# Two w_out chunks and two w_ple_gate chunks as pairs, with seven products for eight in three of eight pairs of k-tiles

## The chip, the core and the metric

The kernel runs on one core of one Trainium2 chip. The time is device microseconds (us) of one execution; lower is better. A core has engines that each work through a list of instructions of their own, in order: PE (TensorE) multiplies matrices, DVE (VectorE) and ACT (ScalarE) work element by element, POOL (GpSimd) does little here, and SP (SyncE) issues transfers between the chip's main memory and the core's own. An instruction waits until what it reads is ready and what it overwrites is no longer needed; whatever stands behind it in the same list waits with it.

## What is computed

One transformer layer for 256 tokens of width 2048, in float32. Cut to what matters here:

```python
z = split_cols(h @ w_in[i])
# three kinds of attention give o_fox, o_nsa, o_dsa
g_fox, g_nsa, g_dsa = jnp.split(jax.nn.sigmoid(z['gate']), 3, axis=-1)
mixed = (g_fox * (o_fox.reshape(B, S, -1) @ w_br_fox[i])
         + g_nsa * (o_nsa.reshape(B, S, -1) @ w_br_nsa[i])
         + g_dsa * (o_dsa.reshape(B, S, -1) @ w_br_dsa[i]))
h = layer_norm(ALPHA * h + mixed @ w_out[i], ln1_g[i], ln1_b[i])
a, b = jnp.split(h @ w_ffn_in[i], 2, axis=-1)
h = layer_norm(ALPHA * h + (jax.nn.silu(a) * b) @ w_ffn_out[i], ln2_g[i], ln2_b[i])
h = h + (p[i] @ w_ple_in[i]) * jax.nn.sigmoid(h @ w_ple_gate[i])
```

The matrices `w_out` and `w_ple_gate` are 2048x2048. Both their products are worked in four chunks of 512 output columns.

## The kernel before

**Halves.** A float32 product is made of three: each operand is split by `halves` into a high half (an ACT copy to the type `fp32r`, L144) and a low half (a DVE subtraction, L145), and PE adds high x high, low x high and high x low in its accumulator (L212 to L214). Weights come as `raw` tiles of two 128-row k-tiles, 128x1024, loaded by SP (L155 in `weight_group`); their halves are `whi` and `wlo`. The matmul that reads a `wlo` is the third of its three, so PE can start a tile with `whi` alone and needs `wlo` two matmuls later.

**One chunk at a time.** `gemm` makes 512 columns for all 256 tokens: 16 k-tiles, two halves of 128 tokens, three matmuls each: 96 matmuls 128x512. Its results lie in two accumulators `acc`. `w_out` runs so in `add_and_norm`: four chunks; after each the residual is added straight from the accumulator (`residual`, L881, a scalar_tensor_tensor on DVE that writes `y`) and its statistics are taken. After chunk 1 come the parameters of the norm and `gated_input`, two small products with `w_ple_in`. `w_ple_gate` runs so in a loop at the end of `build`: after each chunk ACT takes the sigmoid (L1042), DVE multiplies by `ple` (L1043) and adds `y` (L1044), and SP stores.

**Two chunks at a time.** `pair_gemm` makes two chunks of 512 columns at once, and takes the 16 k-tiles by pairs, p = 0 to 7. A pair of k-tiles is a 2x2 matter: two k-tiles, two halves of the tokens, two chunks. In an ordinary pair it takes eight products of three matmuls. In a pair that is in `F.pairs`, here `SEVEN` = (2, 4, 6), it takes seven, by sums and differences of the blocks: 5 x 24 + 3 x 21 = 183 matmuls instead of 192. The differences of the weights are made by DVE (L278 to L280, tiles `raw`), and all are split into halves (`wd`, three blocks wide, and two `wt`); the sums of the other operand are made once by `Forms.put` (tiles `xs`, split into `xf`) and serve every chunk. Four of the seven products gather in accumulators of their own, `m[1]`, `m[5]`, `m[6]`, `m[7]`, over the three seven-pairs; behind the last seven-pair ACT copies `m[1]` and DVE adds the others (L298 to L301, tiles `g`), while PE goes on with the next ordinary pair; at the very end the four ordinary accumulators are added (L305). In the kernel before, the gate chunks (`two_gates`) and 20 of 22 chunks of `w_ffn_in` (`next_chunk`) run in this way, 39 seven-pairs in all.

**What sets the order.** The program writes the steps one after the other, and a scheduler puts them into each engine's list, ahead of their place in the text where their operands and a free buffer allow it. Buffers come from rotating pools: `raw`, `whi`, `wlo` from `wp`, `raw8` of the pairs from a pool of their chunk, wide tiles of the tag `k4` from `k4` and `k4b`. A load waits until its buffer's last reader is done, and SP issues loads in order.

Of the kernel before, what the change touches and what calls it, by code (L numbers as in the profile page):

```python
# [10 lines left out]
F32 = mybir.dt.float32  # L11
# [20 lines left out]
SEVEN = (2, 4, 6)  # L32
# [89 lines left out]
def build(ctx: ExitStack, tc: tile.TileContext, A: dict):  # L122
# [120 lines left out]
    def pair_gemm(a, b, X, F, kt, pool, banks):  # L243
# [15 lines left out]
        def split(src, name, pool, n, **kw):  # L259
            hi, lo = (pool.tile([P, n, 512], F32R, name=f"w{name}{x}", tag=f"w{name}{x}", **kw) for x in ("hi", "lo"))  # L260
            halves(src, hi, lo)
            return [(hi[:, i, :], lo[:, i, :]) for i in range(n)]

        for p in range(np_):
            raw = pool.tile([P, 4, 512], F32, name="raw8", bufs=3)
            nc.sync.dma_start(raw[:, 0:2, :], b[:, 2 * p:2 * p + 2, :])
            nc.sync.dma_start(raw[:, 2:4, :], a[:, 2 * p:2 * p + 2, :])
            x = [[tuple(t[:, hs[h]] for t in X(2 * p + k)) for k in range(2)] for h in range(2)]
            if p not in F.pairs:
                w = [split(raw[:, 2:4, :], "", wp, 2), split(raw[:, 0:2, :], "", wp, 2)]  # L270
# [7 lines left out]
            DVE.tensor_tensor(t[0], raw[:, 0:1, :].broadcast_to([P, 2, 512]), raw[:, 1:3, :], op=ALU.subtract)  # L278
            DVE.tensor_sub(t[1][:, 0, :], raw[:, 1, :], t[0][:, 1, :])
            DVE.tensor_sub(t[1][:, 1, :], raw[:, 3, :], t[1][:, 0, :])  # L280
            b22, b11, b21 = split(raw[:, 1:4, :], "d", pool, 3, bufs=1)
            t3, t1 = split(t[0], "t", pool, 2)
            t2, t4 = split(t[1], "t", pool, 2)
# [11 lines left out]
            if stop:  # L295
# [5 lines left out]
                DVE.tensor_add(e[0][:, 1, :], e[0][:, 1, :], m[5])  # L301
            tick()
        for h in range(2):
            for j in range(2):
                DVE.tensor_add(e[h][:, j, :], e[h][:, j, :], c[h][j])  # L305
# [524 lines left out]
    def two_gates(n):  # L830

        e = pair_gemm(A["gate"][n], A["gate"][4 + n], X, F, KT, gq, (acc_tile, sc_tile))
        for h in range(2):
            ACT.activation(e[h], e[h], AF.Sigmoid)
# [4 lines left out]
        return {"fox": [t[:, 0, :] for t in e], "nsa": [t[:, 1, :] for t in e], "dsa": [g[:, h, :] for h in range(2)]}  # L839

    mixT = Halves()
    for n in range(4):
        G = two_gates(n) if n else {name: [g[:, h, :] for h in range(2)] for name, g in G0.items()}
        if n == 3:
# [6 lines left out]
            halves(mix2, *mixT.t[2])  # L851
        mix = None
# [69 lines left out]
    def add_and_norm(src, X, kt, old, params_of, extra, T, long, spare, first=None):  # L922

        stats = new_stats()
        for n in range(4):
# [29 lines left out]
    def x_tile(n):  # L955
# [7 lines left out]
                 lambda: gated_input(k4, 0, ep), later, LONG1, [k4] * (LONG1 - 4))  # L963
# [15 lines left out]
    def next_chunk(c, pool, banks):  # L979
        e = pair_gemm(A["ffn_in"][c], A["ffn_in"][11 + c], hT, F, KT, pool, banks)  # L980
        for h in range(2):
            ACT.activation(e[h][:, 0, :], e[h][:, 0, :], AF.Silu)
# [111 lines left out]
```

## Time and profile before

| | us |
|---|---|
| median of three runs | 1592.51 |
| the three runs | 1591.29, 1592.51, 1595.47 |
| the profiled execution | 1591.16 |
| its span, first to last instruction | 1589.4 |
| PE busy in the span | 1577.2 (99%) |
| DVE busy | 1110.2 (70%) |
| ACT busy | 785.2 (49%) |

The profile is one execution. Its own time lies 1.76 us above its span and 1.35 us below the median of the three runs. "Busy" is the time in which an engine had an instruction under way. Matmuls overlap: one begins before the last has ended, so what a matmul costs is read from the distance between the starts of two, not from its duration; the same holds, to a lesser degree, for instructions of DVE and ACT. Views used below: the page; the waits (who waited, for what, how long in all, how often, the longest); the windows (busy time of each engine in a stretch); the timeline (each instruction with start and duration, and in brackets the idle time ahead of it).

In the span, the products with `w_br_*` of the last chunk end at about 678 us, those with `w_out` fill 676 to about 775, `w_ffn_in` and `w_ffn_out` follow, and `w_ple_gate` runs from about 1500 to the end at 1589.4.

### The profile page before, as it was taken

To read this page: it belongs to the slowest core of one execution; us is meant where nothing else is said; L and a number is where in the kernel's file an instruction comes from. 1 tells how busy PE (TensorE), PEld (TensorE's weight loads), DVE (VectorE), ACT (ScalarE), POOL (GpSimd) and SP (SyncE) were. 2 spreads that over 40 slices of the span, in tenths; PEclk is the share of its full clock that TensorE was granted. 3 is DMA by queue.
4 is the path that set the end of the run, shared out by engine and by line. 5 is a ranking of instruction groups with operands and counts; after the bars stand their busy time and mean duration, and the time that the engine had idled before them with its cause. 6 is when DMAs were issued, how large, how long until landed. Compare 5 with 4: busy or idle time off the path is not lost. (4 is left out here: it accounts for less than half of the span.)

```text
span 1589.4 us, 19951 instructions
## 1 busy us (share of the span) xinstructions
PE 1577.2 (99%) x7464; PEld 1316.6 (83%) x7464; DVE 1110.2 (70%) x1451; ACT 785.2 (49%) x961; POOL 19.0 (1%) x40
## 2 busy tenths in 40 slices
PE   9999999999999999999999999999999999999998
PEld 7778899988888888888788888888888888888787
DVE  5678565554877777556878888888889664544854
ACT  5445455554544545444455555555555544433443
POOL 1000000000000001000000000000000000000000
PEclk9999999999999999999999999999999999999999
DMA  8665644576475655777565656656665976666474
GB/s 273 221 212 170 195 130 128 163 245 217 145 248 166 222 165 184 219 229 218 164 215 203 207 203 224 219 205 202 223 224 179 299 237 197 195 195 201 144 231 131
DMA packets 92754, 319.72 MB, mean 201 GB/s; under 512 B 10608, under 2 KB 11760, under 8 KB 92656
## 3 DMA queue, kind: packets, MB, share of 16 engines
q1 hardware_dynamic: 91376, 314.25, 61.5%
q0 software_dynamic: 1280, 4.20, 1.0%
q8 instruction: 58, 0.95, 0.2%
q14 instruction: 40, 0.33, 0.1%
HBM read 311.58 MB, written 6.82 MB: 200 GB/s over the span
## 5 line engine op out<-in xcount | busy, mean ns | idle before, releaser
L145 DVE TENSOR_TENSOR wlo<-raw,whi 128x1024 fp32r<-128x1024 f32 (+3 forms) x478 | 564.3, 1187 | 393.4 <-ACT whi L144 389.6
L144 ACT ACTIVATE whi<-raw 128x1024 fp32r<-128x1024 f32 (+3 forms) x478 | 492.7, 1032 | 625.3 <-PE acc L213 360.4
L212 PE MATMUL acc<-whi,k4h 128*128 128x512 f32 (+3 forms) x1388 | 533.2, 384 | 1.5 <-ACT k4h L144 1.4
L213 PE MATMUL acc<-whi,k4l 128*128 128x512 f32 (+3 forms) x1388 | 526.2, 379 | 0.6 <-DVE k4l L145 0.6
L214 PE MATMUL acc<-wlo,k4h 128*128 128x512 f32 (+3 forms) x1388 | 525.8, 379 | 0.0
L212 PEld LDWEIGHTS acc<-whi,k4h 128*128 128x128 f32 x1388 | 261.0, 188 | 51.0 <-issue 4.3
L214 PEld LDWEIGHTS acc<-wlo,k4h 128*128 128x128 f32 x1388 | 260.8, 188 | 45.2 <-DVE wlo L145 0.4
L213 PEld LDWEIGHTS acc<-whi,k4l 128*128 128x128 f32 x1388 | 261.2, 188 | 44.7 <-DVE k4l L145 1.3
L255 PE MATMUL acc<-whi,k4h 128*128 128x512 f32 x320 | 125.2, 391 | 0.0
L257 PE MATMUL acc<-wlo,k4h 128*128 128x512 f32 x320 | 124.9, 390 | 0.0
L256 PE MATMUL acc<-whi,k4l 128*128 128x512 f32 x320 | 124.6, 389 | 0.0
L144 ACT ACTIVATE wthi<-raw 128x1024 fp32r<-128x1024 f32 x78 | 82.1, 1054 | 34.0 <-DVE raw L280 24.6
L145 DVE TENSOR_TENSOR wtlo<-raw,wthi 128x1024 fp32r<-128x1024 f32 x78 | 92.1, 1217 | 0.0
L145 DVE TENSOR_TENSOR wdlo<-raw,wdhi 128x1536 fp32r<-128x1536 f32 x39 | 68.4, 1755 | 16.9 <-ACT wdhi L144 16.5
L255 PE MATMUL sc<-whi,k4h 128*128 128x512 f32 x200 | 78.3, 391 | 0.0
L257 PE MATMUL sc<-wlo,k4h 128*128 128x512 f32 x200 | 77.9, 389 | 0.0
L256 PE MATMUL sc<-whi,k4l 128*128 128x512 f32 x200 | 77.8, 389 | 0.0
L144 ACT ACTIVATE wdhi<-raw 128x1536 fp32r<-128x1536 f32 x39 | 58.1, 1490 | 29.1 <-PE acc L256 15.5
L257 PEld LDWEIGHTS acc<-wlo,k4h 128*128 128x128 f32 x320 | 60.1, 188 | 12.4
L256 PEld LDWEIGHTS acc<-whi,k4l 128*128 128x128 f32 x320 | 60.1, 188 | 12.3
L255 PEld LDWEIGHTS acc<-whi,k4h 128*128 128x128 f32 x320 | 60.1, 188 | 12.1
L278 DVE TENSOR_TENSOR raw<-raw 128x1024 f32<-128x1024 f32 x39 | 47.5, 1219 | 6.2 <-DMA raw<-ffn_in 5.4
(307 smaller groups left out, 1483.4 us busy)
## 6 DMA issues: line engine op xcount, KB each, us to landing
raw<-ffn_in SPq DMA_DIRECT2D x176, 512.0 KB, 4.4
raw<-gate SPq DMA_DIRECT2D x96, 512.0 KB, 4.4
raw<-ffn_out SPq DMA_DIRECT2D x88, 512.0 KB, 4.3
raw<-att_c SPq DMA_DIRECT2D x40, 512.0 KB, 4.4
raw<-att_f SPq DMA_DIRECT2D x48, 384.0 KB, 3.3
raw<-w_out SPq DMA_DIRECT2D x32, 512.0 KB, 4.1
raw<-ple_gate SPq DMA_DIRECT2D x32, 512.0 KB, 4.2
g<-cmp SPq DMA_DIRECT2D x16, 512.0 KB, 5.1
```

The lines of the kernel that those rows point to most:

```text
L144: ACT.activation(hi, src, AF.Copy)
L145: DVE.tensor_sub(lo, src, hi.bitcast(F32))
L212: PE.matmul(o, xh[:, c], h, start=(k == 0), stop=False)
L213: PE.matmul(o, xl[:, c], h, start=False, stop=False)
L214: PE.matmul(o, xh[:, c], l, start=False, stop=(k == kt - 1))
L255: PE.matmul(o, xh, h, start=first, stop=False)
L256: PE.matmul(o, xl, h, start=False, stop=False)
L257: PE.matmul(o, xh, l, start=False, stop=stop)
L278: DVE.tensor_tensor(t[0], raw[:, 0:1, :].broadcast_to([P, 2, 512]), raw[:, 1:3, :], op=ALU.subtract)
```

## The change

The first two chunks of `w_out` (0 and 1) and the middle two of `w_ple_gate` (1 and 2) now run by `pair_gemm`. For `w_out` the seven-pairs are (1, 3, 5), for `w_ple_gate` (2, 4, 6). In these two calls (`slots` is given) the weights of a seven-pair lie in tiles of the shared pools `k4` and `k4b`: each raw load is a tile of its own (`rawb` for the second chunk, `rawa` for the first), the one 1024-wide difference becomes two 512-wide ones, and the 1536-wide split of `wd` becomes a 512-wide (`whl`) and a 1024-wide one. `Forms` of `mixT` are made in the last chunk of the mixing, ahead of its `w_br` products; those of `h2T` behind chunk 0 of `w_ple_gate`. For `w_out` a function `mid` adds the residual to each of the four sums behind the last seven-pair, ahead of the ordinary accumulators; statistics, parameters and `gated_input` come after the pair. The gate of an output block is now the function `gated`. In the other uses of `pair_gemm` one sigmoid 1024 wide becomes two 512 wide; `next_chunk` is only written otherwise.

```diff
--- before.py
+++ after.py
@@ -29,7 +29,7 @@
 LONG1, LONG2, LONG3 = 8, 7, 5
 WARM = 9
 
-SEVEN = (2, 4, 6)
+SEVEN, SEVEN_MIX = (2, 4, 6), (1, 3, 5)
 
 STAY, AHEAD = 2, 1
 NCMP = 15
@@ -240,7 +240,8 @@
         def __call__(self, p, j):
             return self.t[p][:, 0, j, :], self.t[p][:, 1, j, :]
 
-    def pair_gemm(a, b, X, F, kt, pool, banks):
+    def pair_gemm(a, b, X, F, kt, pool, banks, mid=None, slots=None):
...
 
         def split(src, name, pool, n, **kw):
-            hi, lo = (pool.tile([P, n, 512], F32R, name=f"w{name}{x}", tag=f"w{name}{x}", **kw) for x in ("hi", "lo"))
+            tag = "k4" if pool is slots else f"w{name}%s"
+            hi, lo = (pool.tile([P, n, 512], F32R, name=f"w{name}{x}", tag=tag.replace("%s", x), **kw) for x in ("hi", "lo"))
             halves(src, hi, lo)
             return [(hi[:, i, :], lo[:, i, :]) for i in range(n)]
 
         for p in range(np_):
-            raw = pool.tile([P, 4, 512], F32, name="raw8", bufs=3)
-            nc.sync.dma_start(raw[:, 0:2, :], b[:, 2 * p:2 * p + 2, :])
-            nc.sync.dma_start(raw[:, 2:4, :], a[:, 2 * p:2 * p + 2, :])
+            if slots:
+                rb, ra = (slots.tile([P, 2, 512], F32, name=f"raw{x}", tag="k4") for x in "ba")
+            else:
+                raw = pool.tile([P, 4, 512], F32, name="raw8", bufs=3)
+                rb, ra = raw[:, 0:2, :], raw[:, 2:4, :]
+            nc.sync.dma_start(rb, b[:, 2 * p:2 * p + 2, :])
+            nc.sync.dma_start(ra, a[:, 2 * p:2 * p + 2, :])
             x = [[tuple(t[:, hs[h]] for t in X(2 * p + k)) for k in range(2)] for h in range(2)]
             if p not in F.pairs:
-                w = [split(raw[:, 2:4, :], "", wp, 2), split(raw[:, 0:2, :], "", wp, 2)]
+                w = [split(ra, "", wp, 2), split(rb, "", wp, 2)]
                 for h in range(2):
                     for j in range(2):
                         for k in range(2):
@@ -275,12 +281,22 @@
                 tick()
                 continue
             t = [wp.tile([P, 1024], F32, name="raw", bufs=3).rearrange("p (k w) -> p k w", k=2) for _ in range(2)]
-            DVE.tensor_tensor(t[0], raw[:, 0:1, :].broadcast_to([P, 2, 512]), raw[:, 1:3, :], op=ALU.subtract)
-            DVE.tensor_sub(t[1][:, 0, :], raw[:, 1, :], t[0][:, 1, :])
-            DVE.tensor_sub(t[1][:, 1, :], raw[:, 3, :], t[1][:, 0, :])
-            b22, b11, b21 = split(raw[:, 1:4, :], "d", pool, 3, bufs=1)
-            t3, t1 = split(t[0], "t", pool, 2)
-            t2, t4 = split(t[1], "t", pool, 2)
+            if slots:
+                DVE.tensor_sub(t[0][:, 0, :], rb[:, 0, :], rb[:, 1, :])
+                DVE.tensor_sub(t[0][:, 1, :], rb[:, 0, :], ra[:, 0, :])
+            else:
+                DVE.tensor_tensor(t[0], raw[:, 0:1, :].broadcast_to([P, 2, 512]), raw[:, 1:3, :], op=ALU.subtract)
+            DVE.tensor_sub(t[1][:, 0, :], rb[:, 1, :], t[0][:, 1, :])
+            DVE.tensor_sub(t[1][:, 1, :], ra[:, 1, :], t[1][:, 0, :])
+            if slots:
+                hl = slots.tile([P, 2, 512], F32R, name="whl", tag="k4")
+                halves(rb[:, 1, :], hl[:, 0, :], hl[:, 1, :])
+                b22 = hl[:, 0, :], hl[:, 1, :]
+                b11, b21 = split(ra, "d", slots, 2)
+            else:
+                b22, b11, b21 = split(raw[:, 1:4, :], "d", pool, 3, bufs=1)
+            t3, t1 = split(t[0], "t", slots or pool, 2)
+            t2, t4 = split(t[1], "t", slots or pool, 2)
             first, stop = not m, p == last
             for n in (1, 5, 6, 7):
                 if first:
@@ -299,10 +315,11 @@
                 DVE.tensor_add(e[1][:, 0, :], e[0][:, 1, :], m[7])
                 DVE.tensor_add(e[1][:, 1, :], e[1][:, 0, :], m[5])
                 DVE.tensor_add(e[0][:, 1, :], e[0][:, 1, :], m[5])
+                e = [[(mid or (lambda h, j, o: o))(h, j, e[h][:, j, :]) for j in range(2)] for h in range(2)]
             tick()
         for h in range(2):
             for j in range(2):
-                DVE.tensor_add(e[h][:, j, :], e[h][:, j, :], c[h][j])
+                DVE.tensor_add(e[h][j], e[h][j], c[h][j])
         return e
 
     class Halves:
@@ -831,12 +848,13 @@
 
         e = pair_gemm(A["gate"][n], A["gate"][4 + n], X, F, KT, gq, (acc_tile, sc_tile))
         for h in range(2):
-            ACT.activation(e[h], e[h], AF.Sigmoid)
+            for j in range(2):
+                ACT.activation(e[h][j], e[h][j], AF.Sigmoid)
         ps = gemm(A["gate"][8 + n], X, KT, 512)
         g = g_tile()
         for h in range(2):
             ACT.activation(g[:, h, :], ps[h], AF.Sigmoid)
-        return {"fox": [t[:, 0, :] for t in e], "nsa": [t[:, 1, :] for t in e], "dsa": [g[:, h, :] for h in range(2)]}
+        return {"fox": [t[0] for t in e], "nsa": [t[1] for t in e], "dsa": [g[:, h, :] for h in range(2)]}
 
     mixT = Halves()
     for n in range(4):
@@ -849,6 +867,9 @@
             k4b = part.enter_context(tc.tile_pool(name="k4b", bufs=10, reuse_waits="tile"))
             mixT.add(k4b)
             halves(mix2, *mixT.t[2])
+            F = Forms(k4, k4, SEVEN_MIX)
+            for p in SEVEN_MIX:
+                F.put(p, mixT)
         mix = None
         for name, kt, k0 in (("dsa", 6, 10), ("nsa", 4, 0), ("fox", 6, 4)):
             ps = gemm(A["br_" + name][n], lambda k: O(k0 + k), kt, 512)
@@ -919,10 +940,23 @@
             DVE.scalar_tensor_tensor(y, y, rstd, gb[n][:, 1, :], op0=ALU.mult, op1=ALU.add)
             to_dmajor(T, 4 * n, y, h)
 
-    def add_and_norm(src, X, kt, old, params_of, extra, T, long, spare, first=None):
+    def add_and_norm(src, X, kt, old, params_of, extra, T, long, spare, first=None, pair=None):
 
         stats = new_stats()
-        for n in range(4):
+        if pair:
+            o = [old(j) for j in range(2)]
+
+            def mid(h, j, e):
+                DVE.scalar_tensor_tensor(Y[h][j], o[j][h], ALPHA, e, op0=ALU.mult, op1=ALU.add)
+                return Y[h][j]
+
+            pair(mid)
+            for h in range(2):
+                for j in range(2):
+                    DVE.bn_stats(stats[h][:, j, :], Y[h][j])
+            gb = params_of()
+            extra()
+        for n in range(2 if pair else 0, 4):
             o = old(n)
             if n < 3:
                 ps = gemm(src[n], first if first and n == 0 else X, kt, 512)
@@ -960,7 +994,8 @@
     E = []
     later = Later(k4)
     add_and_norm(A["w_out"], mixT, KT, x_tile, lambda: params("ln1_g", "ln1_b", k4b),
-                 lambda: gated_input(k4, 0, ep), later, LONG1, [k4] * (LONG1 - 4))
+                 lambda: gated_input(k4, 0, ep), later, LONG1, [k4] * (LONG1 - 4),
+                 pair=lambda mid: pair_gemm(A["w_out"][0], A["w_out"][1], mixT, F, KT, None, (acc_tile, sc_tile), mid, k4))
     hT = later.x
 
 
@@ -978,10 +1013,10 @@
 
     def next_chunk(c, pool, banks):
         e = pair_gemm(A["ffn_in"][c], A["ffn_in"][11 + c], hT, F, KT, pool, banks)
-        for h in range(2):
-            ACT.activation(e[h][:, 0, :], e[h][:, 0, :], AF.Silu)
-            DVE.tensor_mul(e[h][:, 0, :], e[h][:, 0, :], e[h][:, 1, :])
-        return [e[h][:, 0, :] for h in range(2)]
+        for g, u in e:
+            ACT.activation(g, g, AF.Silu)
+            DVE.tensor_mul(g, g, u)
+        return [g for g, _ in e]
 
     spilled = {}
 
@@ -1029,20 +1064,31 @@
     add_and_norm(A["ffn_out"], actT, 44, lambda n: (Y[0][n], Y[1][n]), lambda: params("ln2_g", "ln2_b", k4),
                  lambda: gated_input(k4, 2, k4), later, LONG2, [k4b] * (LONG2 - 4), first=act_first)
     h2T = later.x
-    for n in range(4):
-        kw = {}
-        if n == 0:
-            kw = dict(sizes=[[2] * LONG3], spare=[k4b] * (LONG3 - 4))
-        elif n == 3:
-            kw = dict(sizes=[[2]] * 5 + [[2, 2, 2]], parts=2)
+
+    def gated(n, h, c, s, o):
+
+        ACT.activation(s, o, AF.Sigmoid)
+        DVE.tensor_mul(s, s, E[n][:, h, c])
+        DVE.tensor_add(s, s, Y[h][n][:, c])
+        nc.sync.dma_start(A["out"][h, :, n * 512 + c.start:n * 512 + c.stop], s)
+
+    F = Forms(k4b, k4b, SEVEN)
+    for n in (0, 1, 3):
+        if n == 1:
+            e = pair_gemm(A["ple_gate"][1], A["ple_gate"][2], h2T, F, KT, None, (acc_tile, sc_tile), slots=k4b)
+            for h in range(2):
+                for j in range(2):
+                    gated(1 + j, h, slice(0, 512), e[h][j], e[h][j])
+            continue
+        kw = dict(sizes=[[2]] * 5 + [[2, 2, 2]], parts=2) if n else dict(sizes=[[2] * LONG3], spare=[k4b] * (LONG3 - 4))
         ps = gemm(A["ple_gate"][n], h2T, KT, 512, **kw)
         s = g_tile()
         w = 512 // (len(ps) - 1)
         for h, c, o in [(0, slice(0, 512), ps[0])] + [(1, slice(i * w, (i + 1) * w), o) for i, o in enumerate(ps[1:])]:
-            ACT.activation(s[:, h, c], o[:, :c.stop - c.start], AF.Sigmoid)
-            DVE.tensor_mul(s[:, h, c], s[:, h, c], E[n][:, h, c])
-            DVE.tensor_add(s[:, h, c], s[:, h, c], Y[h][n][:, c])
-            nc.sync.dma_start(A["out"][h, :, n * 512 + c.start:n * 512 + c.stop], s[:, h, c])
+            gated(n, h, c, s[:, h, c], o[:, :c.stop - c.start])
+        if n == 0:
+            for p in SEVEN:
+                F.put(p, h2T)
 
 
 # ---- launch: one core; the arrays laid out as the kernel loads them ----
```

**DVE in the first two chunks of w_out.** Before, from chunk 0 to the residual of chunk 1 (`wlo`: low halves of weights; `y`: the residual):

```order
L145 TENSOR_TENSOR wlo<-raw,whi 128x1024 x7
L881 SCALAR_TENSOR_TENSOR y<-xt,acc 128x512 x2
L882 BN_STATS stats_5923<-y 128x6
L882 BN_STATS stats_5924<-y 128x6
L145 TENSOR_TENSOR wlo<-raw,whi 128x1024 x8
L881 SCALAR_TENSOR_TENSOR y<-xt,acc 128x512 x2
```

Now, at the end of pair 5, the last seven-pair (`wtlo`: low halves of its differences; `g`: the sums of `m`; the first `wlo` is pair 6's):

```order
L145 TENSOR_TENSOR wtlo<-raw,wthi 128x1024
L950 SCALAR_TENSOR_TENSOR y<-xt,g 128x512
L145 TENSOR_TENSOR wtlo<-raw,wthi 128x1024
L314 TENSOR_TENSOR g<-g,sc 128x512
L315 TENSOR_TENSOR g<-g,sc 128x512
L316 TENSOR_TENSOR g<-g,sc 128x512
L317 TENSOR_TENSOR g<-g,sc 128x512
L950 SCALAR_TENSOR_TENSOR y<-xt,g 128x512 x3
L145 TENSOR_TENSOR wlo<-rawa,whi 128x1024
L145 TENSOR_TENSOR wlo<-rawb,whi 128x1024
```

Four sums and three residuals now stand between the last `wtlo` of the seven-pair and the first `wlo` of the pair that follows it on PE.

**ACT at the change from chunk 0 to chunk 1 of w_ple_gate.** Before (`g<-acc` is the sigmoid of chunk 0):

```order
L144 ACTIVATE k4h<-sc 128x4x128 x3
L144 ACTIVATE whi<-raw 128x1024
L144 ACTIVATE k4h<-sc 128x4x128
L144 ACTIVATE whi<-raw 128x1024 x5
L1042 ACT_TABLE_LOAD
L1042 ACTIVATE g<-acc 128x512 x2
```

Now (`xf`: the halves of the forms; `rawa`, `rawb`: the weights of the pair):

```order
L144 ACTIVATE whi<-raw 128x1024 x2
L144 ACTIVATE xf<-xs 128x512 x3
L1070 ACT_TABLE_LOAD
L1070 ACTIVATE g<-acc 128x512 x2
L144 ACTIVATE whi<-rawa 128x1024
L144 ACTIVATE whi<-rawb 128x1024
```

Three of the five `whi` that stood ahead of the sigmoid were chunk 1's; now none of the pair's stands ahead of it.

**DVE at the same place.** Before:

```order
L145 TENSOR_TENSOR wlo<-raw,whi 128x1024
L145 TENSOR_TENSOR k4l<-sc,k4h 128x4x128
L145 TENSOR_TENSOR wlo<-raw,whi 128x1024 x5
L1043 TENSOR_TENSOR g<-g,ple 128x512 x2
L1044 TENSOR_TENSOR g<-g,y 128x512 x2
L145 TENSOR_TENSOR wlo<-raw,whi 128x1024 x8
```

Now:

```order
L145 TENSOR_TENSOR xf<-xs,xf 128x512
L1071 TENSOR_TENSOR g<-g,ple 128x512 x2
L1072 TENSOR_TENSOR g<-g,y 128x512 x2
L145 TENSOR_TENSOR wlo<-rawa,whi 128x1024
L145 TENSOR_TENSOR wlo<-rawb,whi 128x1024
```

The first `wlo` of the pair stands behind the gate of chunk 0, where three of chunk 1 stood ahead of it. At the end of the last seven-pair of this pair of chunks, pair 6, DVE has the same four sums (L314 to L317) ahead of the first `wlo` of pair 7, without residuals.

## Rows read from the trace of the kernel before

**Rows 1.** The page: busy time of each engine, share of the span, instructions.

```profile
PE 1577.2 (99%) x7464; PEld 1316.6 (83%) x7464; DVE 1110.2 (70%) x1451; ACT 785.2 (49%) x961; POOL 19.0 (1%) x40
```

**Rows 2.** Waits of PE, the longest: us in total, times, longest.

```profile
PE sc L535 <- DVE ra L528: 1.7, 1, 1.7
```

**Rows 3.** Windows: length, busy PE, PEld, DVE, ACT, POOL, clock, DMA share, GB/s.

```profile
1000.00:1100.00 100.00, 100.00 (x452) 82.87 (x451) 87.46 (x89) 55.91 (x57) 0.00 (x0) 1.00 0.63 216
1510.00:1520.00 10.00, 10.00 (x45) 8.26 (x44) 6.04 (x7) 6.32 (x8) 0.00 (x0) 1.00 0.75 227
1580.00:1589.40 9.40, 4.81 (x39) 4.53 (x37) 3.08 (x6) 1.36 (x3) 0.00 (x0) 1.00 0.16 58
```

**Rows 4.** Waits of DVE from 640 to 735 us, around the first w_out chunks.

```profile
DVE wlo L145 <- ACT whi L144: 40.6, 30, 3.0
```

**Rows 5.** Timeline of PE, a gate pair: start, duration, engine, instruction.

```profile
608.79 0.39 PE L255 MATMUL acc<-whi,k4h 128*128 128x512 f32 x1
...
611.96 0.39 PE L257 MATMUL acc<-wlo,k4h 128*128 128x512 f32 x1
612.19 0.39 PE L255 MATMUL sc<-wdhi,k4h 128*128 128x512 f32 x1
```

**Rows 6.** Timeline of DVE, end of one ffn pair of chunks.

```profile
1024.87 1.22 DVE L145 TENSOR_TENSOR wlo<-raw,whi 128x1024 fp32r<-128x1024 f32 x1
...
1028.27 0.68 DVE L298 TENSOR_TENSOR g<-g,acc 128x512 f32<-128x512 f32 x1
...
1030.67 0.68 DVE L300 TENSOR_TENSOR g<-g,acc 128x512 f32<-128x512 f32 x1
1031.27 0.68 DVE L301 TENSOR_TENSOR g<-g,acc 128x512 f32<-128x512 f32 x1
```

**Rows 7.** Timeline of PE there: last into m[6]; later the next pair.

```profile
1026.06 0.39 PE L257 MATMUL acc<-wtlo,xf 128*128 128x512 f32 x1
...
1028.10 0.39 PE L257 MATMUL sc<-wlo,k4h 128*128 128x512 f32 x1
```

**Rows 8.** Timeline of DVE: two differences, the second reads the first.

```profile
1000.73 0.69 DVE L279 TENSOR_TENSOR raw<-raw,raw 128x512 f32<-128x512 f32 x1
1001.45 0.69 DVE L280 TENSOR_TENSOR raw<-raw,raw 128x512 f32<-128x512 f32 x1
```

**Rows 9.** Timeline of DVE: a scalar_tensor_tensor and what follows it.

```profile
1503.06 0.75 DVE L918 SCALAR_TENSOR_TENSOR y<-y,mv,gb 128x512 f32<-128x512 f32 x1
1503.72 1.22 DVE L145 TENSOR_TENSOR wlo<-raw,whi 128x1024 fp32r<-128x1024 f32 x1
```

**Rows 10.** Timeline of ACT, end of w_ple_gate chunk 0.

```profile
1516.99 1.28 ACT L1042 ACT_TABLE_LOAD   x1
1518.29 1.15 ACT L1042 ACTIVATE g<-acc 128x512 f32<-128x512 f32 x2
```

**Rows 11.** Timeline of DVE at the same place.

```profile
1508.84 2.57 DVE L145 TENSOR_TENSOR wlo<-raw,whi 128x1024 fp32r<-128x1024 f32 x2 [0.29 <-ACT whi L144]
...
1518.92 1.30 DVE L1043 TENSOR_TENSOR g<-g,ple 128x512 f32<-128x512 f32 x2 [0.69 <-ACT g L1042]
...
1521.34 1.22 DVE L145 TENSOR_TENSOR wlo<-raw,whi 128x1024 fp32r<-128x1024 f32 x1
```

**Rows 12.** Timeline of PE: last matmul of w_ple_gate chunk 0, then chunk 1.

```profile
1518.41 0.39 PE L214 MATMUL acc<-wlo,k4h 128*128 128x512 f32 x1
1518.64 0.39 PE L212 MATMUL acc<-whi,k4h 128*128 128x512 f32 x1
...
1519.09 0.39 PE L214 MATMUL acc<-wlo,k4h 128*128 128x512 f32 x1
```

**Rows 13.** Tile xs, forms: count, ns min/median/max, first and last start.

```profile
L232 DVE TENSOR_TENSOR xs<-k4h,k4l x6: 678/682/683, 423.0 to 795.5; 128x512 f32<-128x512 f32 x6
L234 DVE TENSOR_TENSOR xs<-xs x6: 281/283/292, 425.0 to 801.1; 128x128 f32<-128x128 f32 x6
```

**Rows 14.** The page: loads of w_out, KB each, median us to landing.

```profile
raw<-w_out SPq DMA_DIRECT2D x32, 512.0 KB, 4.1
```

## The prediction, made before the changed kernel ran

> **What bounds the kernel now.** I read the page first: PE is busy 99% of the span [rows 1]. The waits say how little it lacks anything: its longest single wait is 1.7 us, early in attention [rows 2]. The windows say the same of the stretches that matter: PE is busy all of 1000 to 1100 us, where pairs of `w_ffn_in` chunks run, and all of 1510 to 1520 us in `w_ple_gate`, at a granted clock of 1.00, the 2.4 GHz level [rows 3]. So the time is the number of matmuls times their spacing, plus whatever makes PE wait. DVE is the engine to watch: in the pairs it is busy 87% [rows 3], while around the first `w_out` chunks it waits 40.6 of 95 us for the `whi` of ACT [rows 4]. It has room there on average. The question is what stands in its list at the moments when PE needs something.
>
> **What is saved.** Two pairs of chunks, three seven-pairs each, three matmuls less in each: 18 matmuls. Fifteen spacings lie between 608.79 and 612.19, so one is 0.2267 us [rows 5], and 18 are 4.1 us. A wrong spacing would matter little: the Trainium skill, page "TensorE: Matmul & The Clock Gate", section "Wait — 56ns, not 53.3ns?", gives 0.2157 us for 512 columns at the full clock. By that the saving would be an estimated 3.9 us; the row is measured here and stands. The seven-pairs' differences, splits and the three forms cost DVE and ACT time, which is free as long as PE is fed, as it is in the ffn pairs.
>
> **The end of the last seven-pair of w_out.** Here I expect the largest loss. Behind the last matmul into `m[6]` PE has two matmuls left of pair 5 and two of pair 6 that need only `whi`; the next is the first that reads pair 6's `wlo`. It is due 5 x 0.2267 = 1.13 us after the start of the last into `m[6]`. In an ffn pair of the kernel before that `wlo` was split long ago: it started at 1024.87 and ended 1026.09, ahead of 1026.06 + 0.39, when the sums could begin, and PE read it at 1028.10 without waiting; the first sum came at 1028.27 [rows 6, 7]. In the new order of `w_out` the four sums and three residuals stand ahead of it, and DVE takes its list in order. From the start of the last matmul into `m[6]`: 0.39 until it is done [rows 7]; the sums start 0.72 apart where one reads the result of the one before [rows 8] and 0.60 where not [rows 6]: 0.72 + 0.72 + 0.60 + 0.72; a residual takes 0.66 until the next can start [rows 9], three take 1.98; the `wlo` itself 1.23; two handovers between engines about 0.05 each (the product with `ple` starts 0.05 after the first half of the sigmoid's 1.15 us [rows 10, 11]). That is 6.5 us, less 1.13: **PE waits 5.3 us** (4.4 if nothing depends and the sums run 0.60 apart, 5.8 if ACT's `whi` is late too).
>
> **The start of the pair in w_ple_gate.** Before, the last matmul of chunk 0 started at 1518.41 and chunk 1 went on at 1518.64, reading its first `wlo` at 1519.09 [rows 12]; the `whi` and `wlo` had been made ahead of the sigmoid. Now they stand behind it on ACT, and behind the gate's four instructions on DVE. In the trace the gate's products start at 1518.92 and the next `wlo` at 1521.34 [rows 11]; it would end at 1522.57, and PE reads it 3.5 us after 1519.09. On top, the three forms stand ahead of the table load on ACT: the last `wlo` of chunk 0 ends at 1511.41 [rows 11], three forms of 0.68 + 4 x 0.28 + 0.68 [rows 13] are 7.4 us, or 1518.9; the last 0.7 of that is not waited for by ACT, so its table load of 1.28 us could end at 1519.5 where the sigmoid could start at 1518.8 [rows 10]. By starts instead of durations the forms are quicker, so 0 to 0.7, and I take 0.4: **3.9 us** (3.2 to 4.6).
>
> **The end of pair 6 there.** The same chain without residuals: 0.39 + 0.72 + 0.72 + 0.60 + 0.60 + 1.23 + 0.1 = 4.4; PE has six matmuls here, 1.36: **3.0 us** (2.4 to 3.5).
>
> **Smaller parts.** Four places have no such chain. The transposes of the last mix now stand seven matmuls into the pair, with the prework of pair 1 ahead of the sums on DVE: 0 to 1 us, I take 0.3. Chunk 3 of `w_ple_gate` has ten gate instructions of DVE ahead of its third `wlo`: 0 to 1, I take 0.3, since PE has pair 7 and two groups to do in the meantime. The forms of `mixT` stand in a stretch where DVE waits two fifths of the time [rows 4]: nothing, at most 1. Two sigmoids for one in `two_gates`, and statistics behind the pair: nothing, since nothing on PE reads them soon.
>
> **Sum.** -4.1 + 5.3 + 3.9 + 3.0 + 0.3 + 0.3 = +8.7 us. The profiled execution would go from 1591.16 to 1599.9; it stands 1.35 under the median of the runs, so the median goes from 1592.51 to **1601.2**, +0.55%. A measurement of this kernel can tell about 0.3%, 4.8 us, from no change. With all low ends it is 1592.5 - 4.1 + 10.0 = 1598.4, with the high ones 1592.5 - 4.1 + 13.9 + 3 = 1605.3.
>
> **The rivals.**
> *The saving stands.* PE never waits, as in the pairs of before, which feed it through 39 seven-pairs [rows 3]. This holds if the sums wait for no matmul as late as I say, or if the `wlo` of the next pair were ahead of them. Time: 1592.5 - 4.1 = 1588.4, faster, but within 0.3%. Against it: the list of DVE has the seven instructions ahead of that `wlo`, and the first of them reads what the last matmul into `m[6]` writes. 10%.
> *Only the ends of the pairs cost.* If ACT gets to the pair's `whi` ahead of the last sigmoid's end and DVE runs the gate in its shadow, the start of the `w_ple_gate` pair costs under 1 us, or one of the two ends is half as dear: 1592.5 - 4.1 + 4 to 8 = 1592.4 to 1596.5. For it: PE's due times are worked out to a few tenths only. 17%.
> *Loads come late as well.* In the new calls a raw tile takes a slot of `k4` or `k4b` that a matmul of an earlier pair must free, and lands 4.1 us later [rows 14]. If a slot comes free one pair of k-tiles late, a pair's 21 matmuls, 4.8 us, do not cover 4.1 + 1.23 for a split, and each of the six seven-pairs could wait 0.4 to 1 us: 2.4 to 6 us more, 1604 to 1607. It decides from the point at which the landing comes later than the start of the pair before. 11%.
> *The clock falls.* So far the granted clock was 1.00 everywhere, also in the window that holds the last 4.5 us, in which PE has nothing to do [rows 3]. Should a wait of 3 to 5 us drop it to 1.2 GHz, and it stayed there for as long as the wait had lasted, half of 5.3 + 3.9 + 3.0 us would be lost again, up to 6.1 us: 1603 to 1607. The Trainium skill, page "TensorE: Matmul & The Clock Gate", section "Part 1: The HAM clock gate", says that the idle state is 1.2 GHz and that activity releases it; by that rule the time is this rival's. The trace does not bear it out at its end, and holds no other idle time as long. 12%.
>
> **How the numbers follow.** The main case has 50%, 1598 to 1604.5. Rivals two to four lie on both sides of it. The low end of the range reaches down into the second rival, 1593, the high one into the third and fourth, 1607; outside lie the first rival, a little of the second, and the worst of the others, together under 20%. Faster by over 0.3% means under 1587.7: only the first rival with some luck, 4%. Within 0.3% means up to 1597.3: the rest of the first, the second, and a little of the main case, 24%. Slower: 72%.
>
> **What would show it.** In the changed trace PE should show three idle gaps: one of some 5 us ahead of the third matmul of pair 6 of `w_out`, put down to DVE `wlo`; one of some 4 us in the first three matmuls of the `w_ple_gate` pair, part to ACT `whi`, part to DVE `wlo`; one of some 3 us ahead of pair 7 there. Between them PE is busy at a spacing of 0.227. If there are none, the order of DVE's list is not what decides, and I am wrong in the main step; if the gaps lie elsewhere, at the starts of seven-pairs with a DMA as releaser, the third rival holds; if the clock in the windows behind the gaps is under 1.00, the fourth.

## The result and the profile after

The changed kernel takes 1604.63 us (1602.85 to 1605.40), the kernel before 1591.90 us in runs beside it: the ratio is 1.0086 [1.0074, 1.0099], slower by 12.7 us. The forecast was +8.7 us. The span of the profiled execution went from 1589.4 to 1603.6 us, the mean granted clock from 1.000 to 0.995.

PE has 18 matmuls less than in [rows 1]; the page:

```profile
PE 1581.3 (99%) x7446; PEld 1316.8 (82%) x7446; DVE 1155.8 (72%) x1539; ACT 798.4 (50%) x987; POOL 18.1 (1%) x40
```

The waits of PE, longest first (who waited, for what, us in all, times, the longest), answer to [rows 2], where no wait was over 1.7 us:

```profile
PE acc L258 <- DVE wlo L145: 6.9, 3, 4.1
PE acc L256 <- ACT whi L144: 3.2, 3, 1.9
```

All six stand in three places. The first is the end of the last seven-pair of `w_out`; timeline of PE from the last matmul of pair 5:

```profile
707.67 0.39 PE L258 MATMUL acc<-wtlo,k4h 128*128 128x512 f32 x1
708.66 0.50 PE L256 MATMUL acc<-whi,k4h 128*128 128x512 f32 x1 [0.60 <-ACT whi L144]
709.00 0.40 PE L257 MATMUL acc<-whi,k4l 128*128 128x512 f32 x1
713.50 0.63 PE L258 MATMUL acc<-wlo,k4h 128*128 128x512 f32 x1 [4.10 <-DVE wlo L145]
713.92 0.63 PE L256 MATMUL acc<-whi,k4h 128*128 128x512 f32 x1
...
717.25 0.40 PE L258 MATMUL acc<-wlo,k4h 128*128 128x512 f32 x1
```

The timeline of DVE there shows what `wlo` stood behind: four sums (L314 to L317) and three residuals (L950).

```profile
707.65 0.69 DVE L314 TENSOR_TENSOR g<-g,sc 128x512 f32<-128x512 f32 x1 [0.82 <-PE sc L258]
...
709.70 0.68 DVE L317 TENSOR_TENSOR g<-g,sc 128x512 f32<-128x512 f32 x1
710.41 1.90 DVE L950 SCALAR_TENSOR_TENSOR y<-xt,g 128x512 f32<-128x512 f32 x3
712.23 1.22 DVE L145 TENSOR_TENSOR wlo<-rawa,whi 128x1024 fp32r<-128x1024 f32 x1
```

At 0.227 us a matmul, the L258 was due three distances behind 707.67, at 708.35, and came at 713.50: 5.1 us late. From then on the distance is 0.427 us for eight matmuls, not 0.227: the nine distances from 713.50 to 717.25 take 3.75 us where 2.04 would do. The same at the start of the `w_ple_gate` pair, against [rows 12]:

```profile
1523.74 0.39 PE L214 MATMUL acc<-wlo,k4h 128*128 128x512 f32 x1
1526.06 0.79 PE L256 MATMUL acc<-whi,k4h 128*128 128x512 f32 x1 [1.93 <-ACT whi L144]
1526.64 0.63 PE L257 MATMUL acc<-whi,k4l 128*128 128x512 f32 x1
1528.29 0.79 PE L258 MATMUL acc<-wlo,k4h 128*128 128x512 f32 x1 [1.02 <-DVE wlo L145]
```

The third place is the end of pair 6 there. PE, and below it ACT, whose `whi` waited for a load:

```profile
1565.95 0.40 PE L258 MATMUL acc<-wtlo,k4h 128*128 128x512 f32 x1
1567.05 0.50 PE L256 MATMUL acc<-whi,k4h 128*128 128x512 f32 x1 [0.70 <-ACT whi L144]
1569.61 0.50 PE L258 MATMUL acc<-wlo,k4h 128*128 128x512 f32 x1 [1.82 <-DVE wlo L145]
```
```profile
1565.94 1.06 ACT L144 ACTIVATE whi<-rawa 128x1024 fp32r<-128x1024 f32 x1 [2.12 <-DMA rawa<-ple_gate]
```

The windows show the clock (stretch and its length; busy time and count of PE, PEld, DVE, ACT, POOL; granted clock; DMA share; GB/s), against 1.00 in all of [rows 3]; 0.50 is the 1.2 GHz level, and a number between 0.50 and 1.00 mixes the two levels:

```profile
700.00:710.00 10.00, 8.79 (x38) 6.65 (x36) 4.68 (x7) 3.55 (x4) 0.00 (x0) 1.00 0.75 288
710.00:720.00 10.00, 6.50 (x21) 5.19 (x22) 7.48 (x10) 3.58 (x4) 0.00 (x0) 0.83 0.48 160
1520.00:1530.00 10.00, 7.05 (x25) 4.99 (x24) 7.95 (x14) 7.12 (x9) 0.00 (x0) 0.80 0.28 77
1530.00:1540.00 10.00, 10.00 (x39) 8.10 (x39) 8.96 (x11) 5.53 (x6) 0.00 (x0) 0.85 0.80 273
1570.00:1580.00 10.00, 10.00 (x44) 8.30 (x43) 9.57 (x14) 4.92 (x7) 0.00 (x0) 0.83 0.43 133
```

From 1530 to 1540 PE is busy all the time, and yet 39 matmuls are counted, where 10 us at 0.227 hold 44. This is what the sum lacked:

| term, us | forecast | trace |
|---|---|---|
| 18 matmuls | -4.1 | -4.1 |
| transposes of the last mix | +0.3 | +0.8 |
| wait, end of pair 5, `w_out` | +5.3 | +5.1 |
| wait, start of the `w_ple_gate` pair | +3.9 | +3.5 |
| wait, end of pair 6 there | +3.0 | +3.0 |
| chunk 3 | +0.3 | 0 |
| matmuls 0.427 apart behind the three waits | a rival | +1.7, +2.6, +1.7 |
| sum | +8.7 | +14.3 (spans: +14.2) |

Wait and slow matmuls are worked out for all three places as above. At the start of the `w_ple_gate` pair the third matmul came 3.9 us late, as forecast; 0.4 of that is the slow distance behind the first matmul and stands in the last row but one. The time lies in the range, 3.4 us over the forecast and 0.1 us above the main case's 1598 to 1604.5; the medians differ by 1.5 us less than the two spans.

That the table closes to 0.1 us is partly luck: it holds the two pairs only. Between them and ahead of them the two traces differ too: up to 591 us the new one is 1.2 us shorter, in `w_ffn_in` 0.7 us, and in `w_ffn_out`, which the change doesn't touch, it is 1.8 us longer, by two waits that the old one has not:

```profile
1294.11 0.50 PE L212 MATMUL acc<-whi,k4h 128*128 128x512 f32 x1 [0.43 <-ACT whi L144]
1295.56 0.50 PE L214 MATMUL acc<-wlo,k4h 128*128 128x512 f32 x1 [0.72 <-DVE wlo L145]
```

### The profile page after: what moved, and what is told of

The parts are those of the page before. It is cut to its first block, busy times and chain, and to the rows that moved or that the text cites. A ratio compares the mean times of both kernels' runs of the same rounds, so it can differ in the third digit from the quotient of the medians.

```text
span 1603.6 us, 20021 instructions
## 1 busy us (share of the span) xinstructions
PE 1581.3 (99%) x7446; PEld 1316.8 (82%) x7446; DVE 1155.8 (72%) x1539; ACT 798.4 (50%) x987; POOL 18.1 (1%) x40
## 5 line engine op out<-in xcount | busy, mean ns | idle before, releaser
L145 DVE TENSOR_TENSOR wlo<-raw,whi 128x1024 fp32r<-128x1024 f32 (+3 forms) x446 | 525.6, 1186 | 337.2 <-ACT whi L144 332.8
L144 ACT ACTIVATE whi<-raw 128x1024 fp32r<-128x1024 f32 (+3 forms) x446 | 458.1, 1030 | 565.3 <-PE acc L213 272.5
L212 PE MATMUL acc<-whi,k4h 128*128 128x512 f32 (+3 forms) x1260 | 483.2, 384 | 1.4 <-ACT k4h L144 1.0
L213 PE MATMUL acc<-whi,k4l 128*128 128x512 f32 (+3 forms) x1260 | 476.4, 378 | 0.6 <-DVE k4l L145 0.6
L214 PE MATMUL acc<-wlo,k4h 128*128 128x512 f32 (+3 forms) x1260 | 476.0, 378 | 0.7 <-DVE wlo L145 0.7
L258 PE MATMUL acc<-wlo,k4h 128*128 128x512 f32 x400 | 157.9, 397 | 6.9 <-DVE wlo L145 6.9
L256 PE MATMUL acc<-whi,k4h 128*128 128x512 f32 x400 | 159.2, 398 | 3.2 <-ACT whi L144 3.2
L257 PE MATMUL acc<-whi,k4l 128*128 128x512 f32 x400 | 158.0, 395 | 0.0
L144 ACT ACTIVATE wthi<-raw 128x1024 fp32r<-128x1024 f32 x90 | 94.9, 1055 | 41.0 <-DVE raw L290 30.4
L145 DVE TENSOR_TENSOR wtlo<-raw,wthi 128x1024 fp32r<-128x1024 f32 x90 | 106.9, 1219 | 4.6 <-ACT wthi L144 4.4
L258 PEld LDWEIGHTS acc<-wlo,k4h 128*128 128x128 f32 x400 | 76.4, 191 | 24.6 <-DVE wlo L145 8.5
L258 PE MATMUL sc<-wlo,k4h 128*128 128x512 f32 x200 | 77.9, 390 | 0.0
```

What stands on the lines that cost most here:

```text
L144: ACT.activation(hi, src, AF.Copy)
L145: DVE.tensor_sub(lo, src, hi.bitcast(F32))
L212: PE.matmul(o, xh[:, c], h, start=(k == 0), stop=False)
L213: PE.matmul(o, xl[:, c], h, start=False, stop=False)
L214: PE.matmul(o, xh[:, c], l, start=False, stop=(k == kt - 1))
L256: PE.matmul(o, xh, h, start=first, stop=False)
```

## The experiments

Each kernel was run beside the kernel before, whose median in these runs lies between 1589.45 and 1591.90 us. A difference between the medians of two changed kernels carries some of that; the ratios don't, and their intervals are about 0.1% (2 us) to either side.

**One pair alone.** One kernel keeps the `w_out` pair and gives `w_ple_gate` its four single chunks back, another the reverse.

> Only the pair of w_out chunks is made by pair_gemm; w_ple_gate runs as before, one chunk at a time. Theory (each gap in PE's work costs its wait and, behind it, matmuls at half the granted clock): nine matmuls less are -2.0 us, the transposes wait 0.8, the end of pair 5 5.0, and some 8 matmuls behind it run at half the clock, 1.6: +5.4 us over the kernel before, and one gap of some 4 us ahead of a wlo in the trace, with a granted clock under 1.00 behind it. Rival (the loss is one of the w_ple_gate pair alone, the gap in w_out being given back later): within 1 us of the kernel before.

> Only the pair of w_ple_gate chunks is made by pair_gemm; w_out runs as before. Theory: -2.0 for nine matmuls, 3.5 for the start of the pair, 3.0 for the end of pair 6, and 2.6 + 1.6 for the matmuls at half the clock behind the two: +8.7 us over the kernel before. Together with the w_out pair alone that makes the change's +14 of the two traces. Rival (the two parts act on each other, through the pools or the loads): the two alone add up to 3 us more or less than both together.

Measured: 1595.98 us, 1.0038 [1.0026, 1.0050], and 1598.41 us, 1.0047 [1.0035, 1.0060], beside 1590.29 us: +5.7 and +8.1. The sum, 13.8, is 1.1 us from the whole change, and by the ratios it is 0.85% for 0.86%. Each pair loses by itself; that one disturbs the other doesn't show.

**Is the lower clock the price of the waits?** Matmuls with a 128x64 tile of zeros and 512 columns of data are put into PE's list where it waits: 3 ahead of the first `whi` of `w_out`'s pair 6 and 17 ahead of its `wlo`, 8 and 6 at pair 0 of `w_ple_gate`, 3 and 8 at its pair 7.

```diff
+        def zeros(o, n, first):
+            for _ in range(n):
+                with tc.issue_after(newest_mm[0]):
+                    newest_mm[0] = PE.matmul(o[:64], zero, X.t[0][0][:, 0:2, :].rearrange("p k t -> p (k t)"), start=first, stop=first).ins
```

> The changed kernel with matmuls by a zero operand put into PE's list where it waits: 3 and 17 in pair 6 of w_out, 8 and 6 in pair 0 of w_ple_gate, 3 and 8 in its pair 7. They add nothing to the sums and end before the operand that PE waits for is ready. Theory (the slow matmuls behind the gaps come from PE having been idle): the granted clock stays at 1.00, matmuls behind the gaps are 0.227 us apart, not 0.427, and the kernel is 4 to 6 us faster than the changed one, 1599 to 1601. Rival (they are slow because the transfers then run at nearly all of their rate, or because the waits draw the clock down whatever PE does): no faster than the changed kernel, 1604 or more, and matmuls 0.427 us apart as before.

Measured: 1599.86 us, 1.0062 [1.0050, 1.0074], against 1.0086 of the changed kernel: 4.8 us by the medians, 3.8 by the ratios. The windows of the same places:

```profile
710.00:720.00 10.00, 8.95 (x39) 6.46 (x40) 8.17 (x10) 5.31 (x6) 0.00 (x0) 1.00 0.61 222
1520.00:1530.00 10.00, 9.80 (x42) 6.68 (x41) 8.05 (x14) 6.79 (x8) 0.00 (x0) 1.00 0.37 105
1530.00:1540.00 10.00, 10.00 (x46) 8.29 (x45) 9.54 (x11) 6.24 (x7) 0.00 (x0) 1.00 0.74 263
```

PE still gets these halves late, but has something to do meanwhile, and the clock stays at 1.00. So the slow matmuls do come from PE's idleness, and not from traffic or from the halves being late.

The 4.8 us are less than the 6.0 us of slow matmuls, and one reason is in the trace: at the end of the `w_out` pair the zeros did not end before the operand was ready. DVE had `wlo` at 714.20, PE was busy with the 17 zeros and read it at 715.55. DVE, then PE:

```profile
712.98 1.22 DVE L146 TENSOR_TENSOR wlo<-rawa,whi 128x1024 fp32r<-128x1024 f32 x1
```
```profile
711.62 4.09 PE L258 MATMUL acc<-k4h,zero 128*64 128x512 f32 x17
715.55 0.39 PE L266 MATMUL acc<-wlo,k4h 128*128 128x512 f32 x1
```

**The sums behind the next `wlo`.** In both pairs the four sums (and `w_out`'s residuals) are issued behind the next pair's `wlo`:

```diff
+                if slots and p == last + 1:
+                    with tc.issue_after(done[1].ins):
+                        e = sums()
```

> The changed kernel with the four sums behind the last seven-pair (and the residuals) issued on DVE behind the wlo of the next pair. Theory (DVE's list makes the end of the pairs late): in w_out PE waits only for the landing of pair 6's weights, about 1.6 us instead of 5.0, and no slow clock behind it; in w_ple_gate about 1.7 instead of 3.0, no slow clock; some of it may come back in chunk 3, whose third weight group now has the gate ahead of it, up to 2. Together 6 to 8 us faster than the changed kernel: 1597 to 1599. Rival (the loads are what is late): the gaps stay as long as they are, 1603 to 1605.

Measured: 1604.39 us, 1.0088 [1.0075, 1.0101]: no gain, where 1597 to 1599 was expected. The waits at both ends shrank to 0.5 and 0.9 us and came back later: for `w_out` in part, 1.5 us ahead of and in the products with `w_ple_in`; for `w_ple_gate` in full. In its chunk 3, PE and then DVE:

```profile
1576.46 0.50 PE L213 MATMUL acc<-wlo,k4h 128*128 128x512 f32 x1 [3.39 <-DVE wlo L144]
```
```profile
1573.38 1.29 DVE L1078 TENSOR_TENSOR g<-g,y 128x512 f32<-128x512 f32 x2
1574.59 0.68 DVE L1077 TENSOR_TENSOR g<-g,ple 128x512 f32<-128x512 f32 x1
1575.19 1.22 DVE L144 TENSOR_TENSOR wlo<-raw,whi 128x1024 fp32r<-128x1024 f32 x1
```

The sums are late, so the gates of chunks 1 and 2 are, and chunk 3's `wlo` stands behind those. A place in DVE's list is not freed by moving its tenant one place down. (The profiled execution is 2.0 us shorter than that of the changed kernel; the medians and the ratios show no gain.)

**The loads.** The loads of `ple_in` and of chunk 3 are issued behind the pair's last load.

> The changed kernel with one move: on SyncE's list, the loads of ple_in (while the w_out pair ends) and those of chunk 3 of w_ple_gate (while the other pair ends) are issued behind the last weight load of the pair instead of ahead of it. Nothing is left out. Theory one (the halves of the last pairs of k-tiles are late through VectorE's list, where 4 sums and 3 residuals stand ahead of wlo): the waits for whi shorten by 0.6 to 0.7 us each, those for wlo hardly, and the kernel gains 0 to 1.5 us against the changed one, 1603 to 1604.6. Theory two (the late load, which waits 8 us in SyncE's list for a free buffer, sets the end): the waits for wlo at both ends go with it, 5.0 + 3.0 us and the slow matmuls behind them, 1594 to 1597.

Measured: 1603.07 us, 1.0083 [1.0070, 1.0097]. Two of the three waits for `whi` are gone; the one for `wlo` in `w_out` is 4.5 us instead of 4.1. The gain, 1.6 us by the medians and 0.5 by the ratios, is not clear of the noise. So what the late loads cost beyond DVE's list is at most that.

**The start of the w_ple_gate pair.** Pair 0 is halved ahead of chunk 0's sigmoid, gate, store and forms, which are now `early`:

```diff
+                if early and p == 0:
+                    with tc.issue_after(done[0].ins), tc.issue_after(done[1].ins):
+                        early()
```

> The changed kernel with one move: at the start of the pair of chunks 1 and 2 of w_ple_gate, the halves whi and wlo of its first pair of k-tiles are made ahead of chunk 0's sigmoid, gate and residual forms on ScalarE and VectorE, and those follow. Nothing is left out. My theory (the wait at this start is a place in two engines' lists, and the slow matmuls behind it are the price of that wait): the wait of 3.5 us and some 2.6 us of matmuls at the lower clock go, so -6 us against the changed kernel, near 1598.5 us, with a granted clock near 1.00 in 1520 to 1540. Rival one (the work that was moved comes back): chunk 0's gate, forms and the second pair's halves are now late, a wait of like size stands one or two pairs further on, and the time stays at 1603 to 1605. Rival two (the slow clock has nothing to do with the wait): the wait goes, the slow matmuls stay, 1601.

Measured: 1609.65 us, 1.0124 [1.0110, 1.0137]: 5 us slower than the changed kernel, where 1598.5 was expected. Timelines of SP, ACT and PE there:

```profile
1526.23 0.94 SPq L1075 DMA_DIRECT2D out<-g  x2
1527.23 0.45 SPq L271 DMA_DIRECT2D rawb<-ple_gate  x1
1527.77 0.41 SPq L272 DMA_DIRECT2D rawa<-ple_gate  x1
```
```profile
1533.61 1.06 ACT L144 ACTIVATE whi<-rawa 128x1024 fp32r<-128x1024 f32 x1 [3.88 <-DMA rawa<-ple_gate]
```
```profile
1534.72 0.80 PE L255 MATMUL acc<-whi,k4h 128*128 128x512 f32 x1 [5.93 <-ACT whi L144]
```

The wait is now one pair further on, and longer: SP's list held the store of chunk 0, which waits for the gate, ahead of pair 1's loads. The next kernel issues those two loads ahead of the store (`ahead.append(fetch(1))` ahead of `early()`).

> The run that halved pair 0 of the w_ple_gate pair ahead of chunk 0's gate was 5 us slower than the changed kernel: its wait moved to pair 1, whose loads were issued at 1527.2 us behind the store of chunk 0, which waits for the gate. This kernel is that one with pair 1's two loads issued ahead of the store on SyncE's list. Nothing is left out. My theory (the start costs what two lists make it cost, VectorE's and then SyncE's): no wait of over 1 us between 1515 and 1545 us, granted clock near 1.00 there, and 6 us under the changed kernel, 1597.5 to 1600 us. Rival one (VectorE has no room there: the forms of the later pairs are now late): a wait of 2 to 6 us before pair 2, 1601 to 1607. Rival two (the load is late for the traffic of its own, not for its place in the list): the wait before pair 1 stays, 1608 to 1610.

Measured: 1601.08 us, 1.0066 [1.0052, 1.0079]: 8.6 us less than with these loads behind the store. The windows from 1520 to 1540 hold 0.41 us of idle time and a clock of 1.00: the start is settled, by places in lists: those on ACT and DVE, which were moved together and can't be told apart, and then SP's. Against the changed kernel it is 3.6 us, not 6, and 1597.5 to 1600 was expected; the transposes wait 1.6 us instead of 0.8, and the end of pair 6, which nothing touched, is slow for longer (14 matmuls 0.427 apart instead of eight):

```profile
1560.00:1570.00 10.00, 6.94 (x19) 4.91 (x19) 8.27 (x10) 4.53 (x5) 0.00 (x0) 0.72 0.47 173
```

**All together.** Both starts and ends, the loads, and what the sums displaced: the gates of chunks 1 and 2 go singly between the halves of chunk 3, the statistics of `w_out` behind those of `ple_in`, and pair 1 of `w_out` behind the last mix. The second kernel adds pair 1's loads ahead of the store.

> The changed kernel with all of the moves in one: pair 0 of the w_ple_gate pair is halved ahead of chunk 0's gate and forms; the loads of ple_in and of chunk 3 stand behind the pair's last load; the four sums at each pair's end are made behind the next pair's wlo; what the sums push back is moved as well (the statistics of w_out's chunks 0 and 1 behind the halves of ple_in's weights, the gates of w_ple_gate's chunks 1 and 2 spread between the halves of chunk 3); and the second pair of the w_out pair is halved behind the mix's last sums. Nothing is left out. My theory (waits are places in VectorE's list, and each wait of 3 us or more brings slow matmuls of like price): with no wait over 1 us left the clock stays near 1.00 and 18 matmuls less show, 1587 to 1590 us, 0.1 to 0.3% under the kernel before. Rival (VectorE has no room there: what is moved returns as a wait somewhere in the next 15 us): 1593 to 1600.

> The kernel with all of the moves in one, 1598.29 us, with pair 1's loads of w_ple_gate issued ahead of chunk 0's store as well. Nothing is left out. Its one wait of over 1 us was that for pair 1's whi, 6.0 us, with some 2.5 us of matmuls at the lower clock behind it. My theory: both go, 8.5 us, and 1589 to 1591 us is left, level with the kernel before to 0.2%; of the 4.1 us that 18 matmuls are worth, four waits of 0.3 to 0.7 us in w_out's chunk 3 (at 754 to 759 us), whose loads stand behind the sums, and shorter ones hold back the most. Rival (the DMA and VectorE work that was packed there comes back as waits further on): 1592 to 1598.

Measured: 1598.29 us, 1.0062 [1.0048, 1.0075], where 1587 to 1590 was expected, its one long wait that of the store (5.98 us, PE, for `whi` of pair 1); and 1590.38 us, 1.0003 [0.9994, 1.0012], with no wait over 1.2 us. Two issues on SP's list are worth 7.9 us by the medians, 9.4 by the ratios, and the change is level with the kernel before.

**Where the last 4 us are.** First `w_out`'s statistics are spread between the halves of chunk 2, then pair 2's loads go ahead of the store too.

> The kernel that came out level with the one before (1590.38 us), with the four statistics of w_out's chunks 0 and 1 spread singly behind the halves of chunk 2's weights instead of all four (2.46 us of VectorE) ahead of the first of them. Nothing is left out. Its last waits in w_out are four of 0.3 to 0.7 us at 754 to 759 us, together some 1.7 us. Theory one (VectorE's list: the statistics hold the first halves of chunk 2 and so the three raw buffers and the loads behind them): the waits go, 1588.5 to 1589.5 us, and the kernel is at or 0.1% under the one before. Theory two (the transfers set the pace there, a piece of weights each 2.3 us from 738 to 759, with the buffers that free up late at 720 us): nothing changes, 1590 to 1591.

> The kernel with the spread statistics, 1590.5 us, with pair 2's two loads of w_ple_gate issued ahead of chunk 0's store as well (there they were issued at 1523.0 us, behind it, and the halves and residuals of pair 2 came late: seven waits of 0.1 to 0.5 us between 1530 and 1537 us, together some 1.5 us). Nothing is left out. Theory one (SyncE's list): those waits go, 1588.5 to 1589.5 us. Theory two (VectorE's list is full there: pair 2's residuals now stand between chunk 0's last halves, and the waits stand there instead): 1590 to 1593 us.

Measured: 1590.50 us, 0.9999 [0.9990, 1.0008], no change: the waits at 755 to 760 us stayed, which fits the second theory, that the transfers of `w_out` set the pace there. In the last version's trace ACT waits for these loads ten times from 735 to 760 us, 12.1 us in all; no run changed the transfers. Then 1588.80 us, 0.9992 [0.9983, 1.0001]. Its windows at the start of the pair have no idle time left:

```profile
1520.00:1530.00 10.00, 10.00 (x45) 8.27 (x45) 9.05 (x18) 5.39 (x7) 0.00 (x0) 1.00 0.48 156
1530.00:1540.00 10.00, 10.00 (x46) 8.27 (x45) 9.61 (x12) 6.20 (x7) 0.00 (x0) 1.00 0.76 281
```

This is the best version run, 1.0 us under the kernel before by the medians, and the interval still holds 1. The matmuls saved are worth 4.1. By the two traces the `w_ple_gate` pair gives 1.6 us of its 2.0, while the stretch from 592 to 764 us, which holds the `w_out` pair, is 0.5 us longer than before: its 2.0 us are lost there again, 1.2 us of them at 755 to 759 us.

## Why the prediction was right, and where its sum was short

**The three waits** came where the prediction put them and in its sizes, 5.1, 3.5 and 3.0 for 5.3, 3.9 and 3.0 us. The releaser of each third matmul is DVE's `wlo`, as it said. At both ends PE waited first for a `whi` whose load was late (0.6 and 0.7 us), which the prediction had only as the upper end of one range; it lies inside the wait for `wlo` and adds nothing to it. Counting DVE's list, instruction by instruction, between the event that releases it and the `wlo` that PE needs, was enough; the kernels with one pair alone bear it out (+5.7 and +8.1). One reading of it is wrong without consequence: in [rows 7] the matmul at 1026.06 is the last into `m[5]`; the last into `m[6]` stands three further on, and the `wlo` that ended at 1026.09 is ahead of it all the same:

```profile
1026.73 0.39 PE L257 MATMUL acc<-wtlo,xf 128*128 128x512 f32 x1
```

**The saving** is counted, 18 matmuls, but shows in no time by itself: the three kernels whose long waits were all taken away come out at 1.0003, 0.9999 and 0.9992, and each interval holds 1.

**The step that failed** is the treatment of the clock. The prediction had it as a rival with 12% and 1603 to 1607 us, and took the main sum without it, because in [rows 3] the window in which PE is idle at the end reads 1.00. That row is one execution, and doesn't say what the next idle time does: in the changed kernel the idle stretch at the end is as long, and falls to 0.80 and 0.50 in its second and third parts:

```profile
1598.00:1600.00 2.00, 1.01 (x9) 0.81 (x7) 0.69 (x3) 0.38 (x1) 0.00 (x0) 1.00 0.38 136
1600.00:1602.00 2.00, 0.00 (x0) 0.00 (x0) 0.35 (x1) 0.00 (x0) 0.00 (x0) 0.80 0.21 70
1602.00:1603.60 1.60, 0.00 (x0) 0.00 (x0) 0.00 (x0) 0.00 (x0) 0.00 (x0) 0.50 0.00 0
```

The rival came true on top of the main case, at 6.0 us where it said up to 6.1. That the totals agree is luck: it let the low clock last as long as the wait, and the price is a third of the wait at the first place, three quarters at the second, a bit over half at the third. The sentence of the Trainium skill that stood beside it ("TensorE: Matmul & The Clock Gate", "Part 1: The HAM clock gate": idle means 1.2 GHz, activity releases it) agrees with the trace: 0.427 us for 0.227 behind each wait, none of it where zeros filled the wait. The term should have stood in the sum, as a range: 1.7 for 5.1, 2.6 for 3.5, 1.7 for 3.0, and 2.9 at this third place in the kernel with the start settled, where the third matmul came 3.5 us late.

**The other rivals.** That loads come late does not hold as a price: moving them gave 1.6 us at most. They do come late at both ends, by the list they are issued on: the loads of `ple_in` and of chunk 3 wait ahead of them for a free buffer. That only the ends cost is ruled out by the rows of the start.

**Smaller parts.** The transposes were 0.8 for 0.3, chunk 3 was nothing for 0.3. Behind the moved sums chunk 3 had the longest single wait of that kernel, 3.4 us: its slack was there only because the sums were early.

## What to carry to other kernels

When work of a pair's end goes to an engine that also prepares the next weights, count what stands ahead of those weights in that engine's list and in the list that issues their loads; a wait is worth its length plus the matmuls at half clock behind it, here 1.7 to 2.9 us behind 3.0 to 5.1. A move within a full list gives the wait to the next in line; follow it to the end, over the engines and over the DMA issues, before the move is priced. A store that waits for a result should not stand on the same queue ahead of loads that PE will soon need: here that cost 7.9 and 8.6 us.

## What the runs showed of the hardware

Behind waits of 3 to 5 us in all the granted clock was 0.50, and matmuls 0.427 us apart: from 713.50 to 716.9, from 1526.06 to 1532.7 (with 1.0 us of waiting in it), and from 1570.4 to 1573.7. In the first two places the first matmul behind the wait is slow already; in the third, PE went on at 1569.61 and slowed at 1570.41. Matmuls with a 128x64 tile of zeros in the wait kept it at 1.00. Shorter waits can do it too, and need not: the kernel that came out level reads 0.83 in 1500 to 1510 us, behind transposes with waits of 0.4 and 0.7 us, where the next version reads 1.00 at the same place with the same waits; why is open. The two, in this order:

```profile
1500.00:1510.00 10.00, 9.29 (x38) 7.19 (x37) 7.12 (x10) 4.19 (x6) 0.00 (x0) 0.83 0.47 164
1500.00:1510.00 10.00, 9.26 (x47) 7.25 (x46) 8.50 (x12) 5.08 (x7) 0.00 (x0) 1.00 0.53 186
```
